# A two-layer decoder trunk on one core: opening, raw chunks, keys' diagonal and the place of an inverse

## The chip, the cores and the metric

The kernel runs on one core of one Trainium2 chip. The time is device microseconds of one execution, lower is better. A core has a matrix engine (TensorE, PE in the profile, with its weight loads as PEld), VectorE (DVE), ScalarE (ACT), GpSimd (POOL) and SyncE (SP), which issues the transfers here. Each engine takes its own instructions in order; they wait for one another through semaphores.

## The reference, cut to what matters

256 tokens of width 2048 go through two layers. All data are float32.

```python
for layer in range(2):
    h = rmsnorm(x, gains[0])
    m = even_mixer(h) if layer == 0 else rwkv7_time_mix(h)
    x = x + rmsnorm(m, gains[1])
    x = x + rmsnorm(swiglu(rmsnorm(x, gains[2])), gains[3])

def even_mixer(h):
    q, k, v, u = split(h @ w_in)          # 4 x 1024 columns
    return concat(diff_attention(q, k, v), s5(u)) @ w_out

def rwkv7_time_mix(x):                    # 32 heads of 64
    r, k, v = (mixed(x, j) @ w for j, w in ...)
    decay = exp(-exp(-softplus(-(w0 + tanh(xw @ w1) @ w2)) - 0.5))
    a = sigmoid(a0 + (xa @ a1) @ a2)
    # state S per head, over the 256 steps:
    # S = S * decay + (S @ -kk) outer (kk * a) + v outer k;  y = S @ r
```

The kernel computes the last recurrence in chunks of 64 steps. Each chunk and head needs the inverse T of a triangular 64x64 matrix made from the keys.

## The kernel before

**Weights.** They lie in memory as 776 chunks of eight 128x128 blocks (512 KB) in the order of use. `chunk_load` (L362 to L368) loads a chunk into `wr`; ScalarE rounds it into `wh` (L367) and VectorE subtracts, `wl` = `wr` − `wh` (L368). Each block is then multiplied in three passes (high by high, high by low, low by high) on L305. Each of the three tiles has three buffers. Some small tiles in the second mixer are taken "raw": `wr` alone, as one fp32 multiplication, without L367 and L368.

**Order.** A scheduler orders the instructions by priorities, but in the strict parts TensorE keeps program order. Whatever an engine waits for in its queue holds up all behind it.

**First mixer** (`even`). x and the first weights are loaded in the order of the table LX. x times its gain is split into 16 pairs of tiles `Z`; the same tiles of x are squared on ScalarE (L534), added on GpSimd (L536), and eight small matmuls give the norm. Four tiles of u go through the first eight chunks (`k_outer`). Then come the tiles of the list SEQ: v, q with k, u 4, u 5, and so on, one tile being two chunks. Beside it run the setup of the S5 layer (a long chain of small operations on VectorE, then tables S on GpSimd, L1001 to L1031), its products (VectorE L1059, GpSimd L1062 and L1063), and attention, which needs q and k copied out by VectorE (L711).

**Second mixer.** `rwkv_keys` goes through 16 head pairs j. For each, `gates` (L1568 to L1582) makes the decays and gates with ScalarE, VectorE and GpSimd; `pair` multiplies the keys. GpSimd copies a part of E (shown as H) into a block diagonal `bd` (L1629), TensorE multiplies it with the rest, VectorE masks the result into `ak` (L1633), and it is stored (L1635). After every eight pairs, `inverse` reads the stored `ak` into X (tiles XI, L1651) and runs one chain of 60 dependent VectorE operations (L1661, L1662) between an opening product (L1655) and a closing one (L1666), then stores the two diagonal quarters of the inverses. `inverse2` loads them again into A and W (tiles XI, L1681 to L1683), multiplies them in two steps of small matmuls, and stores the off-diagonal quarter (L1702). In a chunk, T is read back (L1836) and first used in the matmul shown as gs,T.

The call `slot("XI", 2, ...)` gives tiles from a ring of two buffers: X and XT of `inverse`, A and W of `inverse2`, all with the same name. The calls stand in this order: inverse of the first half after pair 8, inverse2 of the first half after the last pair, the first values (`wv`, group 0), inverse of the second half. Then `rwkv_values` starts with 20 units of fill work (values of the other groups) and the chunks; inverse2 of the second half comes in its seventh chunk.

Of the kernel before, what the change touches and what calls it, by code (L numbers as in the profile page):

```python
# [18 lines left out]
P = 128  # L19
T = 256  # L20
DM = 2048
# [17 lines left out]
I1 = 16  # L39
# [7 lines left out]
LX = ((0, 2), (0, 0), (2, 2), (4, 4), (1, 0), (8, 4), (2, 0), (12, 4))  # L47
# [12 lines left out]
BE = "g"  # L60
# [152 lines left out]
class Prog:  # L213
    def __init__(self, ctx, tc, d, layouts, dbg=None, stop=99):
# [4 lines left out]
        self.ahead = {}  # L219
# [31 lines left out]
    def load_const(self, key, t):  # L251
        lay, width = self.lay[key]
        self.nc.sync.dma_start(t, self.d[key])
        return {n: t[:, o:o + w] for n, (o, w) in lay.items()}
# [91 lines left out]

    def gated(self, ins):
# [10 lines left out]
    def chunk_load(self, c, raw=False, hp=None, pool=False):  # L358
        nc = self.nc
        with self.tc.high_priority(offset=HP if hp is None else hp):  # L360
            r = self.wp.tile([P, CB * P], F32, tag="wr", name=f"wr{c}")
            nc.sync.dma_start(r, self.d["wst"][c])  # L362
# [4 lines left out]
            self.gated(nc.scalar.copy(h, r))  # L367
# [43 lines left out]
    def tile(self, w, m, zH, zL, ks=None):  # L411
# [4 lines left out]
        for a, k in enumerate(ks):  # L416
            self.lab(w + str(m // 4))
            self.mmb(ps, w, k, m, zH[k], zL[k], a == 0, a == len(ks) - 1)
# [399 lines left out]
    def even(self):  # L818
        nc, v, gp = self.nc, self.nc.vector, self.nc.gpsimd
        with self.phase("ev"):  # L820
# [10 lines left out]
            ce = self.load_const("ce", self.slot("ce", 1, shape=[P, self.lay["ce"][1]]))  # L831
            acc = Prog.Acc(self)
            for k in range(KD):
                self.split(zH[k], zL[k], x[k], self.gain(0, 0, k))
                acc.add(x[k], k == KD - 1)
            r2 = self.slot("r2", 1, shape=[P, 2])
            _, R, R8 = self.rms_bc(acc.cur, half=0.125, col=r2)
            u = self.arr("U", 1, 8)
            us = self.k_outer([("in", 24 + a) for a in range(4)], zH, zL)
# [5 lines left out]
            mH, mL = self.arr("A", 2, 8, F32R), self.arr("A", 2, 8, F32R)  # L845
            yH, yL = self.arr("Y", 2, 8, F32R), self.arr("Y", 2, 8, F32R)
            lam = self.attn_setup(ce)
# [27 lines left out]
            def main():  # L875
                qk = {}
                for w, h in SEQ:
                    if w == "u":
                        ps = yield from self.tile("in", 24 + h, zH, zL)
                        self.evac_scaled(u[h], ps, R)  # L880
                        st["u"] += 1
                    elif w == "q":
                        q, k = self.tmp("q"), self.tmp("q")
                        ps = yield from self.tile("in", h, zH, zL)
                        self.evac_scaled(q, ps, R8)
                        ps = yield from self.tile("in", 8 + h, zH, zL)
# [93 lines left out]
    def s5_tables(self, cf, qt):  # L980
# [11 lines left out]
        nc.sync.dma_start(flat[:, 1024:], self.d["s5bc"][qt])  # L992
# [375 lines left out]
    def rwkv_consts(self, co):  # L1368
# [15 lines left out]
        co["S"] = cf[:, o + 192:o + 704].rearrange("p (j i) -> p j i", i=P)  # L1384
        self.nc.gpsimd.memset(co["S"], 0.0)
# [9 lines left out]
    def rwkv_keys(self, co, po, xs, x, m):  # L1395
# [128 lines left out]
        for j in range(16):  # L1524
# [24 lines left out]
    def gates(self, co, hid, j, Rd, gw, E):  # L1549
# [18 lines left out]
        v.tensor_scalar(ld, ld, e, e, op0=ALU.mult, op1=ALU.add)  # L1568
        v.tensor_tensor_scan(ld, co["reset"], ld, 0.0, op0=ALU.mult, op1=ALU.add)
        nc.scalar.activation(Pv, ld, AF.Exp)  # L1570
        nc.scalar.activation(iv, ld, AF.Exp, scale=-1.0)
        gp.memset(E[:, :, 0, 0, 0:1], 1.0)
        nc.scalar.activation(E[:, :, 0, 0, 1:], ch(ld)[:, :, :C - 1], AF.Exp)
# [3 lines left out]
        v.tensor_scalar(ta, ta, -0.5, -0.5, op0=ALU.mult, op1=ALU.add)  # L1577
        v.tensor_tensor(E[:, :, 1, 0], ch(ta), ch(iv), op=ALU.mult)
# [13 lines left out]
    def pair(self, co, kk, j, E):  # L1592
# [136 lines left out]
    def rwkv_values(self, co, po, vv):  # L1729
# [31 lines left out]
        self.strict = STRICT  # L1761
        with self.mid():
# [8 lines left out]
        fill(FI)  # L1771
        for s in range(NG * NC_):
# [5 lines left out]
            i2 = self.inverse2(co, po, 1, co["iv"]) if s == S2 else None  # L1778
# [250 lines left out]
```

## Time and profile before

| | |
|---|---|
| median of three runs | 2608.89 us (2600.57 to 2609.81) |
| the profiled execution | 2606.43 us, its span 2604.6 us |
| mean granted TensorE clock | 0.975 |
| busy: TensorE, VectorE, ScalarE, GpSimd | 95%, 63%, 46%, 16% |
| TensorE busy, 1548 to 1577 us | 19.6 of 29 us |

Read first the share of each engine, then a table of stretches: where TensorE is not busy for the whole stretch lies the time that a change can win. A row of a timeline gives the start, the duration, engine, line, operation, the tile written and those read, and in brackets how long the engine stood idle before it and what ended that. A line of a group has the count, the busy time and the mean of one in nanoseconds.

### The profile page before, as it was taken

Reading aid. Unit: us, or ns where it says so; the run is one execution under the profiler, and the core shown is the slowest. Engines: PE = TensorE matmul, PEld = TensorE weight load, DVE = VectorE, ACT = ScalarE, POOL = GpSimd, SP = SyncE. Lnnn points to the kernel's source line nnn. Section 1 sums busy time; section 2 is a strip of 40 time slices with the busy share of each in tenths; the row PEclk is TensorE's granted clock in tenths of the full one; section 3 lists DMA queues with packets and bytes.
Section 4 is the critical chain, followed back from the end, with each engine's and each line's share of the span. In section 5 each row is a group of like instructions: output and inputs, shape, how many; then the busy total and the mean of one; then the engine's idle time right before and its main releaser. Section 6 shows DMA issues by size and latency. Waiting matters only on the chain. (4 is left out here: it accounts for less than half of the span.)

```text
span 2604.6 us, 37350 instructions
## 1 busy us (share of the span) xinstructions
PE 2476.1 (95%) x14155; PEld 2081.8 (80%) x14155; DVE 1632.4 (63%) x2369; ACT 1205.3 (46%) x1808; POOL 408.3 (16%) x664
## 2 busy tenths in 40 slices
PE   7898799999999999998899889999999999999998
PEld 7786688788888888887799778887788888888886
DVE  7888985555555554445569978777555555555444
ACT  5343264644444444444666543443554444444433
POOL 4776621000000000000215630111100000000000
PEclk9898899999999999999999989999999999999999
DMA  6333256655555556664468677765555555555564
GB/s 218 114 114 103 80 178 199 203 187 186 192 187 186 192 186 200 200 224 161 154 216 248 206 224 197 207 200 171 202 187 186 189 190 186 186 190 190 194 206 162
DMA packets 221892, 481.93 MB, mean 185 GB/s; under 512 B 78736, under 2 KB 110736, under 8 KB 219920
## 3 DMA queue, kind: packets, MB, share of 16 engines
q1 hardware_dynamic: 221712, 479.55, 57.5%
q8 instruction: 111, 1.82, 0.3%
q14 instruction: 69, 0.57, 0.1%
HBM read 451.69 MB, written 27.79 MB: 184 GB/s over the span
## 5 line engine op out<-in xcount | busy, mean ns | idle before, releaser
L368 DVE TENSOR_TENSOR wl<-wr,wh 128x1024 fp32r<-128x1024 f32 x760 | 939.8, 1238 | 790.9 <-ACT wh L367 787.6
L367 ACT CAST wh<-wr 128x1024 fp32r<-128x1024 f32 x768 | 806.3, 1051 | 1023.7 <-PE pb L305 729.3
L305 PE MATMUL pg<-wh,Z 128*128 128x512 f32 x1664 | 641.2, 397 | 2.8 <-DVE Z L450 2.4
L305 PE MATMUL pb<-wh,Z 128*128 128x512 f32 x1408 | 554.0, 394 | 4.1 <-DVE Z L450 4.1
L305 PEld LDWEIGHTS pg<-wh,Z 128*128 128x128 f32 x1664 | 313.8, 189 | 72.8 <-issue 3.4
L305 PE MATMUL pg<-wl,Z 128*128 128x512 f32 x832 | 324.9, 391 | 0.4 <-DVE wl L368 0.4
L305 PEld LDWEIGHTS pb<-wh,Z 128*128 128x128 f32 x1408 | 264.9, 188 | 62.4 <-DVE Z L450 5.0
L305 PE MATMUL pb<-wl,Z 128*128 128x512 f32 x704 | 273.7, 389 | 0.0
L305 PE MATMUL pg<-wh,PP 128*128 128x512 f32 x576 | 225.6, 393 | 0.0
L305 PE MATMUL pb<-wh,PP 128*128 128x512 f32 x576 | 225.4, 393 | 0.0
L305 PEld LDWEIGHTS pg<-wl,Z 128*128 128x128 f32 x832 | 157.1, 189 | 34.5 <-DVE wl L368 1.2
L305 PE MATMUL pg<-wh,MX 128*128 128x512 f32 x504 | 174.9, 410 | 2.6 <-DVE X L1816 1.9
L305 PE MATMUL pg<-MX,wh 128*128 128x256 f32 x896 | 168.5, 286 | 6.7 <-ACT wh L367 4.0
L305 PE MATMUL pg<-Z,wh 128*128 128x256 f32 x736 | 146.3, 301 | 15.1 <-ACT wh L367 11.9
L305 PEld LDWEIGHTS pb<-wl,Z 128*128 128x128 f32 x704 | 132.5, 188 | 29.6
L305 PEld LDWEIGHTS pg<-MX,wh 128*128 128x128 f32 x896 | 139.9, 192 | 8.4 <-ACT wh L367 4.7
L305 PEld LDWEIGHTS pg<-Z,wh 128*128 128x128 f32 x736 | 120.5, 204 | 27.1 <-issue 14.8
L305 PE MATMUL pg<-MX,wl 128*128 128x256 f32 x448 | 128.1, 288 | 5.0 <-DVE wl L368 4.9
L305 PEld LDWEIGHTS pb<-wh,PP 128*128 128x128 f32 x576 | 108.2, 188 | 23.4
L305 PEld LDWEIGHTS pg<-wh,PP 128*128 128x128 f32 x576 | 108.2, 188 | 23.4
L500 POOL TENSOR_TENSOR ts<-ts,mhalf 128x1 f32<-128x1 f32 x6 | 3.3, 553 | 759.0 <-DVE ts L499 759.0
L305 PEld LDWEIGHTS pg<-wh,MX 128*128 128x128 f32 x504 | 96.7, 192 | 24.6 <-DVE X L1816 2.8
(429 smaller groups left out, 3639.1 us busy)
## 6 DMA issues: line engine op xcount, KB each, us to landing
wr<-wst SPq DMA_DIRECT2D x776, 512.0 KB, 3.4
dr<-H SPq DMA_DIRECT2D x16, 512.0 KB, 4.2
CH<-dr SPq DMA_DIRECT2D x16, 512.0 KB, 5.2
dr<-X SPq DMA_DIRECT2D x6, 1024.0 KB, 4.8
X<-dr SPq DMA_DIRECT2D x6, 1024.0 KB, 5.6
dr<-ak SPq DMA_DIRECT2D x16, 256.0 KB, 4.1
ln<-lnb SPq DMA_DIRECT2D x8, 512.0 KB, 4.7
S<-s5bc SPq DMA_DIRECT2D x4, 512.0 KB, 6.7
```

Source lines behind the costliest of these rows:

```text
L305: self.pe(self.nc.tensor.matmul(out, lhsT, rhs, start=start, stop=stop))
L367: self.gated(nc.scalar.copy(h, r))
L368: self.gated((nc.gpsimd if pool else nc.vector).tensor_tensor(l, r, h.bitcast(F32), op=ALU.subtract))
L500: self.nc.gpsimd.tensor_tensor(r, ms, self.mhalf[:, 0:1], op=ALU.pow)
```

## The change

Four parts.

1. **Opening.** A memset and 54 bf16 matmuls on a zeroed tile stand before the first real matmul, TensorE is strict from there, the splits of x are issued four steps ahead of the chunks, and chunk 1 is loaded before more of x. The norm comes from x by rows (two more loads of 1 MB, two ScalarE squares with an accumulated sum) instead of 16 squares, 14 additions and eight small matmuls. The constants `ce` and the S5 weights are tied behind chunks 5, 6 and 7.
2. **Raw chunks.** The first eight k-steps of ten tiles (u 4 to 7, q 0 to 2, k 0 to 2) are multiplied as fp32 from `wr` and from eight copies of x times gain (ScalarE, L887 of the new kernel, tiles Y). Ten chunks lose their cast and their subtraction.
3. **Keys.** `bd` is copied by ScalarE. In `gates` a VectorE operation becomes a ScalarE identity and two become one: 32 fewer on VectorE, 16 more on ScalarE.
4. **Inverse.** `inverse2` of the first half moves from the end of the keys, ahead of the first values, into the start of `rwkv_values`, behind the inverse of the second half, in three steps with 10, 5 and 5 units of fill work between. The condition I1 goes.

```diff
-LX = ((0, 2), (0, 0), (2, 2), (4, 4), (1, 0), (8, 4), (2, 0), (12, 4))
+LX = ((0, 2), (0, 0), (2, 2), (1, 0), (4, 4), (2, 0), (8, 4), (12, 4))
+W0 = 54
+NRAW = 3
-BE = "g"
+BE = "a"
...
+            z = (raw[k], None) if k < len(raw) else (zH[k], zL[k])
+            self.mmb(ps, w, k, m, *z, a == 0, a == len(ks) - 1)
...
+            self.warm(W0, cold)
+            for t in range(2):
+                self.behind(nc.scalar.activation(rows[t], rows[t], AF.Square, accum_out=ss[:, t:t + 1]), 4 + t)
...
-                        ps = yield from self.tile("in", 24 + h, zH, zL)
+                        ps = yield from self.tile("in", 24 + h, zH, zL, raw=raw)
-                        ps = yield from self.tile("in", h, zH, zL)
+                        ps = yield from self.tile("in", h, zH, zL, raw=raw if h < NRAW else [])
...
-        v.tensor_scalar(ld, ld, e, e, op0=ALU.mult, op1=ALU.add)
+        nc.scalar.activation(ld, ld, AF.Identity, bias=1.0)
-        v.tensor_scalar(ta, ta, -0.5, -0.5, op0=ALU.mult, op1=ALU.add)
-        v.tensor_tensor(E[:, :, 1, 0], ch(ta), ch(iv), op=ALU.mult)
+        v.scalar_tensor_tensor(E[:, :, 1, 0], ch(ta), 1.0, ch(iv), op0=ALU.add, op1=ALU.mult)
...
-            if j == I1:
-                with self.mid():
-                    list(self.inverse2(co, po, 0, iv))
-        if I1 > 15:
-            with self.mid():
-                list(self.inverse2(co, po, 0, iv))
         for _ in self.values(vv, 0, Vs[:, 0]):
             pass
         with self.mid():
-            co["iv"] = self.inverse(co, po, 1)
+            co["iv"] = [iv, self.inverse(co, po, 1)]
...
+        i2 = self.inverse2(co, po, 0, co["iv"][0])
+        with self.mid():
+            next(i2)
+        fill(FI // 2)
+        with self.mid():
+            next(i2)
+        fill(FI // 4)
+        with self.mid():
+            list(i2)
+        fill(FI // 4)
         with self.mid():
             cur = self.chunk_in(co, 0, 0, V)
...
-        fill(FI)
```

Where instructions move, three places. First SyncE's queue at the inverses. Before, around the end of the first values (XI1428 and XI1429 are the first inverse's tiles, XI1538 and XI1539 are A and W of the first inverse2):

```order
L1665 DMA dr1202_11618<-XI1428_13653 64x32x32 x2
L362 DMA wr457_15063<-wst 128x1024
L1669 DMA dr1432_13728<-XI1429_13654 64x1024
L1681 DMA XI1538_14621<-dr1200_11616 32x16x32 x4
L362 DMA wr458_15081<-wst 128x1024
L1682 DMA XI1538_14621<-dr1432_13728 32x16x32
L1683 DMA XI1539_14622<-dr1202_11618 32x16x32
```

and, at the same place in the changed kernel, where XI1528 and XI1529 are the second inverse's tiles, and XI1539 and XI1540 now are A and W:

```order
L371 DMA wr462_15053<-wst 128x1024
L1702 DMA dr1191_11441<-XI1528_14575 64x32x32 x2
L1706 DMA dr1532_14650<-XI1529_14576 64x1024
L1718 DMA XI1539_14670<-dr1188_11438 32x16x32
L1719 DMA XI1539_14670<-dr1420_13540 32x16x32
L1720 DMA XI1540_14671<-dr1190_11440 32x16x32
```

The loads of A and W stood behind the first inverse's stores; they now stand behind the second inverse's.

Second, VectorE's queue there. Before, after the last `ak` (MU and MV belong to the first chunk, XI1544 to the second inverse):

```order
L1633 TENSOR_TENSOR ak1536_14611<-pa1537_14614,M1195_11605 128x512
L368 TENSOR_TENSOR wl458_15084<-wr458_15081,wh458_15083 128x1024
L1944 COPY fs1600_15337<-M1195_11605 128x8
L1854 TENSOR_TENSOR MU1559_15030<-pa1558_15025,M1195_11605 64x512
L1857 TENSOR_TENSOR MV1557_15018<-pa1558_15025,M1195_11605 64x4x64 x2
L1655 TENSOR_TENSOR XI1544_14919<-XI1544_14919,dl1547_14926 128x1024
```

and now (XI1528 is the second inverse's X):

```order
L1670 TENSOR_TENSOR ak1524_14417<-pa1525_14420,M1183_11426 128x512
L1764 COPY X1236_12129<-pg1527_14428 128x512
L379 TENSOR_TENSOR wl458_14861<-wr458_14858,wh458_14860 128x1024
L1990 COPY fs1588_15143<-M1183_11426 128x8
L379 TENSOR_TENSOR wl459_14917<-wr459_14914,wh459_14916 128x1024
L1692 TENSOR_TENSOR XI1528_14575<-XI1528_14575,dl1531_14582 128x1024
```

The second inverse stood behind the first chunk's MU and MV, with weight subtractions among its operations; it now stands ahead of them, with none between its operations.

Third, VectorE's queue in the first mixer. Before, at the first S5 products (s, L1059) and the copy of the first q (L711):

```order
L1059 TENSOR_TENSOR s2226_1061<-pg224_1055,S119_611 128x512
L733 SCALAR_TENSOR_TENSOR sm170_733<-sm169_731,sm161_713 128x2
L1059 TENSOR_TENSOR s2227_1062<-pg224_1055,S119_611 128x512
L1059 TENSOR_TENSOR s2228_1069<-pb225_1056,S119_611 128x512
L1059 TENSOR_TENSOR s2229_1070<-pb225_1056,S119_611 128x512
L733 SCALAR_TENSOR_TENSOR sm171_735<-sm170_733,sm161_713 128x2
L736 TENSOR_SCALAR sm172_737<-sm160_712 128x2
L711 TENSOR_TENSOR q185_908<-pg187_910,n31_211 128x256
```

and now, where the same products are L1101 and the copy is L723:

```order
L379 TENSOR_TENSOR wl19_1099<-wr19_1096,wh19_1098 128x1024
L1017 TENSOR_TENSOR k24_452<-sm105_618,sm99_607 128x32
L379 TENSOR_TENSOR wl21_1225<-wr21_1222,wh21_1224 128x1024
L723 TENSOR_TENSOR q173_929<-pg175_931,n23_449 128x256
L1037 TENSOR_SCALAR s177_968<-S176_966 128x256
L1171 TENSOR_REDUCE sm143_719<-t142_717 128x2
L733 TENSOR_SCALAR sm147_724<-sm143_719 128x2
L1101 TENSOR_TENSOR s2214_1062<-pg212_1056,S106_623 128x512
```

The copy of the first q has moved ahead of the first S5 products; the subtractions of chunks 18 and 20 are gone from there, and the end of the S5 setup (L1017) stands between those of 19 and 21.

More of the change, by code (lines that the diff above doesn't have):

```diff
@@ L218, in __init__ @@
         self.strict, self.xw = False, []
-        self.ahead = {}
+        self.ahead, self.chunks = {}, {}
         self.alias = {}
@@ L345, in after, with behind @@
                                reason="order")
+    def behind(self, ins, c):
+        for a in self.chunks[c]:
+            if a.ins.engine == ins.ins.engine:
+                self.after(ins.ins, a.ins)
     def gated(self, ins):
@@ L830, in even, with part @@
             zH, zL = self.arr("Z", 4, 16, F32R), self.arr("Z", 4, 16, F32R)
[L831 to L839 removed]
+            self.strict = STRICT
+            u = self.arr("U", 1, 8)
+            cold = u[7][:, :P].bitcast(BF16)
+            gp.memset(cold, 0.0)
+            self.warm(W0, cold)
+            r2, ss = self.slot("r2", 1, shape=[P, 2]), self.slot("ssx", 1, shape=[P, 2])
+            xr = [self.mslots() for _ in range(2)]
+            rows = self.halves(xr)
+            steps = self.k_steps([("in", 24 + a) for a in range(4)], zH, zL)
+            def part(k):
+                self.split(zH[k], zL[k], x[k], self.gain(0, 0, k))
+            for k in range(4):
+                part(k)
+            for k in range(KD):
+                us = next(steps)
+                if k + 4 < KD:
+                    part(k + 4)
+                if k in (6, 8):
+                    t = k // 2 - 3
+                    self.behind(nc.sync.dma_start(rows[t], self.d["cx"][:, t * DM:(t + 1) * DM]), 3 + t)
+                if k == 10:
+                    ce = self.load_const("ce", self.slot("ce", 1, shape=[P, self.lay["ce"][1]]), 5)
+            for t in range(2):
+                self.behind(nc.scalar.activation(rows[t], rows[t], AF.Square, accum_out=ss[:, t:t + 1]), 4 + t)
+            ms = self.tmp("ts", [P, 2])
+            v.tensor_scalar(ms, ss, 1.0 / DM, 1e-6, op0=ALU.mult, op1=ALU.add)
+            gp.tensor_tensor(r2, ms, self.mhalf, op=ALU.pow)
+            self.strict = False
+            pr = self.spread(r2)
+            R, R8 = self.tmp("n"), self.tmp("n")
+            nc.scalar.activation(R, pr, AF.Copy)
+            nc.scalar.activation(R8, pr, AF.Copy, scale=0.125)
             with self.tc.high_priority(offset=SET):
@@ L845, in even @@
             mH, mL = self.arr("A", 2, 8, F32R), self.arr("A", 2, 8, F32R)
+            lam = self.attn_setup(ce)
+            raw = self.arr("Y", 2, 8)
             yH, yL = self.arr("Y", 2, 8, F32R), self.arr("Y", 2, 8, F32R)
-            lam = self.attn_setup(ce)
+            for k in range(8):
+                nc.scalar.activation(raw[k], x[k], AF.Copy, scale=self.gain(0, 0, k))
             st = dict(u=4, qk=[], vn=0, att=0, pv=0, s5=0)
```

38 lines of the change are left out of this document (22 added, 16 removed).

## The prediction

> **What bounds the kernel now.** I read the page first, then the table of busy time by stretches of the span, then in the stretches that the change touches the waits and the timelines of TensorE (PE), VectorE (DVE) and the SyncE queue.
>
> ```profile
> PE 2476.1 (95%) x14155; PEld 2081.8 (80%) x14155; DVE 1632.4 (63%) x2369; ACT 1205.3 (46%) x1808; POOL 408.3 (16%) x664
> ```
>
> TensorE is busy for 95% of 2604.6 us. The profiled execution took 2606.43 us, 1.8 more than its span and 2.5 less than the median, 2608.89. I sum against 2606.43 and add nothing for the 2.5. The table by stretches (length, then busy time of PE, PEld, DVE, ACT, POOL; near the end the clock) shows where the missing 5% lies:
>
> ```profile
> 0.00:43.00 43.00, 29.46 (x202) 28.64 (x202) 32.96 (x84) 24.09 (x48) 12.46 (x23) 0.88 0.68 232
> ...
> 65.00:145.00 80.00, 67.28 (x502) 60.08 (x501) 70.16 (x161) 26.72 (x49) 60.57 (x126) 0.89 0.35 113
> 145.00:360.00 215.00, 184.11 (x1416) 150.22 (x1416) 186.87 (x384) 78.86 (x170) 130.75 (x199) 0.90 0.33 106
> ...
> 1400.00:1548.00 148.00, 134.21 (x1011) 124.12 (x1009) 136.51 (x266) 84.09 (x180) 78.39 (x93) 0.97 0.73 218
> 1548.00:1577.00 29.00, 19.62 (x320) 16.27 (x320) 12.47 (x29) 9.79 (x18) 2.20 (x5) 0.71 0.87 212
> ```
>
> The change touches only these. Idle PE is 13.5 us in the opening, 12.7 up to 145, 30.9 up to 360, 13.8 in the keys, 9.4 around the first inverse: this is all that any part can win, besides the clock. In the first mixer and the keys VectorE is nearly as full as TensorE.
>
> **Opening.** Rows of PE's timeline (start, duration):
>
> ```profile
> 9.07 1.65 PE L305 MATMUL pg<-Z,wh 128*128 128x256 f32 x6 [9.07 <-ACT wh L367]
> 16.46 1.65 PE L305 MATMUL pg<-Z,wh 128*128 128x256 f32 x6 [2.81 <-ACT wh L367]
> 20.20 1.01 PE L305 MATMUL pg<-Z,wl 128*128 128x256 f32 x3 [1.66 <-DVE wl L368]
> 26.91 0.28 PE L305 MATMUL pg<-Z,wl 128*128 128x256 f32 x1
> 27.27 0.28 PE L305 MATMUL pg<-Z,wl 128*128 128x256 f32 x1
> 27.74 0.95 PE L305 MATMUL pb<-inv,n 128*128 128x1 f32 x8
> 28.55 0.95 PE L305 MATMUL pg<-Z,wh 128*128 128x256 f32 x6
> ```
>
> A block of three matmuls takes 0.36 us (26.91 to 27.27), a chunk of eight 2.85. Six matmuls took 1.65 us after the wait of 2.81 and 0.95 us at 28.55, so the second chunk ran at half clock. The change warms PE before the first chunk, takes 16 squares from ScalarE, and drops the eight small matmuls for the norm (27.74 to 28.55, 0.8 us). With the second chunk ready by about 15 us, six more at 2.85 and some 5 us of it still at half clock, the tiles end near 38 instead of 43.03: −5. Everything in the first 43 us that waits for the first weights (9.07) stays. Without any clock gain it is −2.5, with all of it −7.5. The trace lets a gap of 2.81 us throttle the clock. [...]
>
> What the opening wins has to get past the S5 tables. GpSimd's chain of small products starts when VectorE has copied a cosine, runs without a break, and VectorE's S5 products wait for it, with the copy of q queued behind them:
>
> ```profile
> 54.33 0.35 POOL L1001 COPY S<-k 128x8 f32<-128x8 f32 x2 [0.31 <-DVE k L962]
> 85.43 1.29 DVE L1059 TENSOR_TENSOR s<-pb,S 128x512 f32<-128x512 f32 x2 [1.24 <-POOL M L1063]
> 86.88 0.41 DVE L711 TENSOR_TENSOR q<-pg,n 128x256 f32<-128x256 f32 x1
> 87.35 1.65 PE L305 MATMUL pa<-q,q 64*128 64x128 f32 x8 [6.28 <-DVE q L711]
> 123.59 1.65 PE L305 MATMUL pa<-q,q 64*128 64x128 f32 x8 [4.75 <-DVE q L711]
> ```
>
> In the new order the cosine copy stands behind the wl of chunk 17, which needs a buffer that PE frees late in the first values. The values start near 38, six chunks of 2.85 bring that to 55, the cast, the subtraction and ten small operations of 0.2 to 59: 4 to 6 later than 54.33 (I allow 1 either way), though PE is 5 earlier. So the wait of 6.28 at 87.35 grows, by about 2 (bounds 0 and +6).
>
> **Ten chunks in fp32.** The kernel already has this form elsewhere; the rows of it and of what is dropped:
>
> ```profile
> L305 PE MATMUL pg<-MX,wr 128*128 128x256 f32 x128 | 28.1, 380 | 1.2 <-POOL MX L1408 1.2
> L367 ACT CAST wh<-wr 128x1024 fp32r<-128x1024 f32 x768 | 806.3, 1051 | 1023.7 <-PE pb L305 729.3
> L368 DVE TENSOR_TENSOR wl<-wr,wh 128x1024 fp32r<-128x1024 f32 x760 | 939.8, 1238 | 790.9 <-ACT wh L367 787.6
> wr<-wst SPq DMA_DIRECT2D x776, 512.0 KB, 3.4
> ```
>
> Those are 64 blocks (two records each): 28.1/64 = 0.44 us against 0.36, so 80 blocks cost TensorE 80 × 0.08 = +6.4. VectorE loses 10 × 1.24 = 12.4 us, ScalarE 10.5 less eight copies of x. A raw buffer is freed by TensorE instead of VectorE, so the next-but-two load starts late: it has one split chunk and one raw chunk, 2.85 + 3.5 = 6.3 us, for landing (3.4, the last row), cast 1.05 and subtraction 1.24, together 5.7. That just holds; I book 0, with +6 as the bound (ten times 0.6).
>
> What VectorE's relief returns: six of the ten chunks lie before 123.59, 7.4 us, more than the 4.75 waited there. That wait goes (−4.75), two small ones of 0.67 and 0.90 too, and with them some of the clock (0.89 over 80 us, 8.8 us lost; I take 2.5 back). The first mixer up to 145: −5 + 2 + 6.4 − 4.75 − 1.6 − 2.5 = **−5**; bounds −13 and +7. From 145 to 360 nothing is removed; an earlier start moves all alike: 0 (±4).
>
> **Keys.** Rows of the timeline and of the sources:
>
> ```profile
> 1445.28 2.08 PE L305 MATMUL pa<-bd,H 128*128 128x128 f32 x8 [4.72 <-POOL bd L1629]
> L1629 POOL COPY bd<-H x32: 387/486/7919, 1371.2 to 1541.4; 64x256 f32<-64x256 f32 x32
> L1603 ACT COPY KR<-pg x16: 362/370/379, 1366.9 to 1521.9; 128x256 f32<-128x256 f32 x16
> L1568 DVE TENSOR_SCALAR m<-m x16: 232/280/849, 1358.8 to 1515.4; 128x256 f32<-128x256 f32 x16
> L1577 DVE TENSOR_SCALAR m<-m x16: 273/300/1837, 1361.4 to 1520.8; 128x256 f32<-128x256 f32 x16
> ```
>
> The diagonal copies go to ScalarE: 32 × 0.37 = 12 us, and 16 identities of some 0.4 us make 6; with 84 of 148 us busy it holds them. VectorE loses 16 × 0.28 + 16 × 0.30 = 9.3 of 136.5. The 4.72 us wait goes; of the rest (13.8 idle) I take 1.3: **−6**, bounds −13 (all idle) and +4 (copies behind the 1.05 us casts, one in four late by half a microsecond).
>
> **The first half's inverse moved behind the values.** This is the large term. Its two tiles A and W and the tiles X and XT of both inverses share two buffers. Before, A and W came between the two inverses; now the second inverse takes the buffers first. SyncE's queue, which runs in order, now holds the second inverse's stores ahead of the twelve loads of A and W, so TensorE's XI matmuls, held in program order after only 15 fill matmuls, wait for the whole second chain. Before, that chain ran on VectorE under fill work. Rows of the timelines of DVE, SP and PE, and how long the stores of ak took to land, and VectorE's busy time on these tiles from 1560 to 1635 (62 operations of the chain and its memset):
>
> ```profile
> 1537.61 2.03 DVE L1666 TENSOR_TENSOR XI<-XI,dl 64x1024 f32<-64x1024 f32 x1
> 1547.84 0.69 DVE L1633 TENSOR_TENSOR ak<-pa,M 128x512 f32<-128x512 f32 x1 [0.20 <-PE pa L305]
> 1566.51 1.23 DVE L1655 TENSOR_TENSOR XI<-XI,dl 128x1024 f32<-128x1024 f32 x1
> 1560.39 2.27 SPq L1651 DMA_DIRECT2D XI<-dr  x2
> DMA to landing us min/median/max: 2.0/4.1/7.6
> 1560.00:1635.00 75.00, 26.02 (x63) 0.94 0.74 196
> 1550.88 1.35 PE L305 MATMUL pb<-XI 32*32 32x32 f32 x122 [0.79 <-DMA XI<-dr]
> 1552.90 0.75 PE L305 MATMUL pb<-XI 32*32 32x32 f32 x38 [0.68 <-ACT XI L1691]
> 1558.32 0.25 PE L305 MATMUL pb<-XI 32*32 32x32 f32 x1 [4.03 <-issue]
> 1562.77 2.05 PE L305 MATMUL pa<-QB,CH 128*128 128x128 f32 x8 [2.48 <-DMA QB<-dr]
> 1576.99 1.14 PE L305 MATMUL pb<-gs,T 64*64 64x64 f32 x16
> ```
>
> Count from the last ak (1547.84), which the second inverse needs and which stands at the same place in both. To the first use of T (1576.99) it was 29.2 us. Now: ak 0.7; its store lands, 4.1; loads of X to the first operation, 1560.39 to 1566.51, 6.1; the chain 26.0; its last store, twelve loads and TensorE's main run, 1539.64 to 1550.88, 11.3; from there to T, 26.1 less the three waits of 0.68, 4.03 and 2.48, 18.9. Together 67.1: **+38**. The fill work between is the same 39 matmuls, so this is idle. Short end: a store landing in 2, loads usable in 4 and (my estimates both) 15 us behind the XI matmuls: 59, +30. Long end: 7.6 for the store, 13.3 and the full 26.1: 79.8, +50. VectorE is then free of the chain while the first values chunks run; the waits there are short: **−2** (0 to −4).
>
> Sum: 2606.4 − 5 − 6 + 38 − 2 = **2631**, 1% above the median.
>
> **Rivals.**
> - *VectorE is the bound of the first 360 us and of the keys.* It is busy 70.2 of 80, 186.9 of 215 and 136.5 of 148 us. If each microsecond taken from it there is one of time, and the saved waits also hold the clock up: −7.5 opening, −12.4 and as much again in clock and GpSimd's products, −13 keys, −2: −47, against a short stall of +30: **2590**, faster. It decides once the gains pass the stall. For it: the two waits for q behind VectorE's queue. Against: TensorE's idle time up to 145 is 12.7 us, with 6.4 added to it.
> - *A short stall and full gains at half that size*: −24 and +30, **2612**, no change. For it: queued stores often land in 2 us. Against: the chain's 26.0 alone nearly equals all that.
> - *Raw buffers free late*: ten split chunks each late by 0.6 to 1, as VectorE's queue holds wl behind S5 products; opening eaten by GpSimd's tables: +12 over the forecast, **2643**.
> - *The inverse does not wait* (loads served from other buffers): −13, **2593**. The order of the queue rules it out but for a misreading.
>
> **How the numbers follow.** Forecast 0.60, late buffers 0.12, no change 0.15, VectorE's bound 0.09, no wait 0.04. About 0.5% (13 us, so 2595.8 and 2621.9) can be told from no change. Of the forecast's case some 0.06 falls below 2621.9 (bounds of the stall and the gains together). Slower: 0.54 + 0.12 = 0.66; same: 0.06 + 0.15 = 0.21; faster: 0.09 + 0.04 = 0.13. The forecast's own range is 2616 to 2645; with no change and late buffers taken in, 2606 to 2648 leaves out about 0.2.
>
> **What would show it.** After the values' end PE stands idle for some 40 us in one piece, released by DMA XI<-dr or ACT, with VectorE running 62 XI operations without a wl among them. If that gap is under 25 us, the large term is wrong. PE's first S5 wait for q near 85 us still stands, the second near 120 is gone; raw matmuls start 0.22 us apart by record; no wait for bd stands in the keys, or it is put down to ACT. If the first 360 us come out more than 15 us shorter, VectorE was the bound and my step on the opening failed.

## The result and the profile after

The changed kernel takes 2629.86 us (median of four runs, 2628.50 to 2631.28), the kernel before 2607.3 (four runs, 2600.57 to 2609.81). The ratio is 1.0088 with a 95% interval of 1.0076 to 1.0100: slower by 0.9%, where 2631 was forecast. The profiled execution has a span of 2629.4 us against 2604.6, so 24.8 us are to be found.

Four marks divide both spans at places where the kernels do the same: the last matmul of `pg<-wh,A` that waited at the end of the first mixer ("mixer" below), the last `ak`, the first use of T, and the end.

| us | mixer | last ak | first T | span |
|---|---|---|---|---|
| before | 335.57 | 1547.84 | 1576.99 | 2604.6 |
| after | 336.28 | 1541.62 | 1604.13 | 2629.4 |
| after less before, up to here | +0.7 | −6.2 | +27.1 | +24.8 |
| the stretch alone | +0.7 | −6.9 | +33.4 | −2.3 |

First the page's line of busy times, after:

```profile
PE 2478.0 (94%) x14121; PEld 2077.1 (79%) x14121; DVE 1615.7 (61%) x2328; ACT 1214.1 (46%) x1842; POOL 358.0 (14%) x619
```

Each engine's sum is almost the same as before: TensorE 2478.0 against 2476.1. The loss is not more work but waiting. Where it lies, the table of stretches of after shows (length, busy time of PE, PEld, DVE, ACT, POOL, then the clock):

```profile
0.00:35.50 35.50, 31.48 (x241) 28.49 (x242) 21.53 (x57) 24.99 (x42) 1.40 (x10) 1.00 0.88 325
65.00:145.00 80.00, 65.34 (x401) 54.34 (x397) 64.92 (x151) 16.83 (x38) 54.12 (x131) 0.94 0.30 101
145.00:360.00 215.00, 182.42 (x1386) 147.83 (x1385) 183.59 (x382) 76.99 (x168) 128.55 (x198) 0.91 0.32 107
1400.00:1541.00 141.00, 130.91 (x1011) 122.01 (x1010) 131.47 (x244) 97.80 (x219) 57.59 (x69) 0.98 0.75 231
1541.00:1600.00 59.00, 17.05 (x312) 13.56 (x311) 31.26 (x73) 8.05 (x13) 3.61 (x6) 0.62 0.53 128
```

The last row is the large one: 17 of 59 us busy at clock 0.62. The keys (1400 to 1541) hold TensorE 93% busy instead of 91%. Between 65 and 145 VectorE has 5.2 us less to do than before, and TensorE, with 65 of 80, is no fuller for it. TensorE's timeline of after, at the places that the prediction named:

```profile
1.10 8.91 PE L315 MATMUL pa<-U 128*128 128x256 bf16 x54 [1.10 <-POOL U L846]
9.77 0.48 PE L308 MATMUL pg<-Z,wh 128*128 128x256 f32 x2
...
14.36 0.50 PE L308 MATMUL pg<-Z,wh 128*128 128x256 f32 x2 [1.62 <-ACT wh L377]
...
36.37 0.40 PE L308 MATMUL pg<-wh,Z 128*128 128x512 f32 x1
...
81.09 0.93 PE L308 MATMUL pa<-q,q 64*128 64x128 f32 x8 [4.44 <-DVE q L723]
81.95 2.86 PE L308 MATMUL pg<-Y,wr 128*128 128x256 f32 x6
...
123.13 1.23 PE L308 MATMUL pa<-q,q 64*128 64x128 f32 x6 [6.91 <-DVE q L723]
...
336.28 0.50 PE L308 MATMUL pg<-wh,A 128*128 128x512 f32 x1 [2.24 <-DVE q L723]
...
1582.60 0.28 PE L308 MATMUL pb<-XI 32*32 32x32 f32 x2 [36.29 <-DMA XI<-dr]
...
1587.80 1.88 PE L308 MATMUL pb<-XI 32*32 32x32 f32 x122 [1.28 <-DMA XI<-dr]
...
1604.13 1.11 PE L308 MATMUL pb<-gs,T 64*64 64x64 f32 x16 [1.53 <-DMA T<-dr]
```

The opening does what it should: behind the warm-up (1.10) the first matmuls at 9.77 and those behind a wait of 1.62 at 14.36 run at full clock (1.00 in the first row of the table), and the first tiles end at 36.37 where they ended at 43. But the second wait for q stands at 123.13 where it stood at 123.59, and is longer (6.91 against 4.75). By there the opening's gain is gone. At 1582.60 stands the gap the forecast was built on, 36.29 us in one piece, ended by a load of XI. The other engines' timelines of after give its working, VectorE's chain and SyncE's queue:

```profile
1541.62 0.69 DVE L1670 TENSOR_TENSOR ak<-pa,M 128x512 f32<-128x512 f32 x1
1551.05 1.23 DVE L1692 TENSOR_TENSOR XI<-XI,dl 128x1024 f32<-128x1024 f32 x1 [2.16 <-DMA XI<-dr]
1575.22 1.86 DVE L1703 TENSOR_TENSOR XI<-XI,dl 64x1024 f32<-64x1024 f32 x1
1594.93 1.23 DVE L379 TENSOR_TENSOR wl<-wr,wh 128x1024 fp32r<-128x1024 f32 x1 [17.84 <-ACT wh L377]
```

```profile
1546.26 2.06 SPq L1688 DMA_DIRECT2D XI<-dr  x2
1577.12 1.63 SPq L1706 DMA_DIRECT2D dr<-XI  x1
1580.10 0.34 SPq L1718 DMA_DIRECT2D XI<-dr  x1
```

The chain runs from 1551.05 to 1577.08 without anything else on VectorE, its store goes out at 1577.12, and only then, at 1580.10, the loads of A and W that TensorE waits for. SyncE's own waits there are 16.6 us for the chain, with the second inverse's first store at the head of its queue, and 1.3 us for a store to land, in front of the first load of A. Behind the chain VectorE itself idles 17.84 us, to 1594.93, until the next `wh` is cast: ScalarE stands 42.08 us, to 1589.71, for TensorE's XI matmuls and then 3.55 us more for TensorE's weight matmuls (pg) before that cast, so there is nothing to subtract.

### The profile page after: what moved, and what is told of

It is laid out like the page before. It is cut to its first block, busy times and chain, and to the rows that moved or that the text cites. A ratio compares the mean times of both kernels' runs of the same rounds, so it can differ in the third digit from the quotient of the medians.

```text
span 2629.4 us, 37168 instructions
## 1 busy us (share of the span) xinstructions
PE 2478.0 (94%) x14121; PEld 2077.1 (79%) x14121; DVE 1615.7 (61%) x2328; ACT 1214.1 (46%) x1842; POOL 358.0 (14%) x619
## 4 chain that ended last, share of the span: by engine, by line
PE 79%; DVE 10%; ACT 3%; POOL 3%; DMA 2%; issue 2%; SPq 0%; DVEq 0%; ACTq 0%; POOLq 0%
PE pg L308 44%; PE pb L308 32%; DVE wl L379 2%; PE pa L308 2%; DMA wr<-wst 1%; PE pa L711 1%; ACT wh L377 1%; DVE s L1101 1%; DVE XI L1698 1%; DVE M L1123 1%; DVE XI L1699 0%; DVE X L1123 0%; DVE s L1137 0%; ACT MX L1447 0%; DVE sm L1119 0%
## 5 line engine op out<-in xcount | busy, mean ns | idle before, releaser
L379 DVE TENSOR_TENSOR wl<-wr,wh 128x1024 fp32r<-128x1024 f32 x750 | 929.1, 1240 | 826.1 <-ACT wh L377 825.8
L377 ACT CAST wh<-wr 128x1024 fp32r<-128x1024 f32 x758 | 795.9, 1051 | 1015.6 <-PE pb L308 725.6
L308 PEld LDWEIGHTS pb<-wh,Z 128*128 128x128 f32 x1408 | 264.7, 188 | 62.5 <-DVE Z L462 5.0
L308 PEld LDWEIGHTS pg<-wl,Z 128*128 128x128 f32 x832 | 157.1, 189 | 34.5 <-DVE wl L379 1.2
L308 PE MATMUL pg<-Z,wh 128*128 128x256 f32 x576 | 113.3, 296 | 5.3 <-DVE s L1101 3.7
L308 PE MATMUL pg<-wl,PP 128*128 128x512 f32 x288 | 111.8, 388 | 0.0
L308 PE MATMUL pb<-wl,PP 128*128 128x512 f32 x288 | 111.7, 388 | 0.0
```

What stands on the lines that cost most here:

```text
L308: self.pe(self.nc.tensor.matmul(out, lhsT, rhs, start=start, stop=stop))
L377: ins.append(nc.scalar.copy(h, r))
L379: self.gated((nc.gpsimd if pool else nc.vector).tensor_tensor(l, r, h.bitcast(F32), op=ALU.subtract))
```

## The experiments

"Early loads" in the names below means that the loads of A and W stand again between the two inverses. All ratios are to the kernel before, each with its 95% interval. What every run gave at the four marks ("ak to T" is first T less last ak):

| kernel | mixer | last ak | first T | ak to T | span | ratio |
|---|---|---|---|---|---|---|
| before | 335.6 | 1547.8 | 1577.0 | 29.2 | 2604.6 | 1 |
| after | 336.3 | 1541.6 | 1604.1 | 62.5 | 2629.4 | 1.0088 |
| e1_inv_back | 337.0 | 1541.8 | 1576.3 | 34.5 | 2610.3 | 1.0001 |
| e2_inv_only | 338.0 | 1554.3 | 1618.0 | 63.8 | 2641.5 | 1.0120 |
| e3_inv_early_loads | 337.9 | 1545.8 | 1573.3 | 27.5 | 2601.7 | 0.9980 |
| e4_open_keys | 335.6 | 1542.0 | 1577.3 | 35.3 | 2604.4 | 0.9997 |
| e5_inv_back_late_second | 336.4 | 1546.0 | 1576.6 | 30.7 | 2603.1 | 0.9994 |
| e6_early_consts | 336.5 | 1547.5 | 1576.7 | 29.3 | 2607.8 | 0.9997 |
| e7_raw_only | 346.3 | 1563.6 | 1593.7 | 30.1 | 2628.2 | 1.0068 |
| e8_keys_only | 335.7 | 1543.4 | 1574.9 | 31.5 | 2604.1 | 0.9984 |
| e9_keys_early_loads | 339.4 | 1544.2 | 1571.6 | 27.4 | 2597.6 | 0.9963 |
| e10_open_only | 335.9 | 1551.7 | 1580.9 | 29.2 | 2610.1 | 1.0000 |
| e11_no_first_scan | 329.0 | 1536.3 | 1564.6 | 28.3 | 2592.2 | 0.9950 |
| e12_raw_late_copies | 341.2 | 1556.3 | 1583.5 | 27.2 | 2619.7 | 1.0053 |

A mark alone is good to about 2 us either way: before, e2, e8 and e9 have the same first mixer, and the mark is 335.6, 338.0, 335.7 and 339.4. What many rows share is firmer than any one.

**e1: after, with the first half's inverse2 put back.**

```diff
+        with self.mid():
+            list(self.inverse2(co, po, 0, iv))
         for _ in self.values(vv, 0, Vs[:, 0]):
...
-        i2 = self.inverse2(co, po, 0, co["iv"][0])
-        with self.mid():
-            next(i2)
-        fill(FI // 2)
...
+        fill(FI)
```

> The changed kernel with one part undone: inverse2 of the first half stands again at the end of the keys, ahead of the first values. Theory (shared ring of two buffers): the whole of the step at the inverses, -6 to +25.5 against before in the two traces, goes, so about 31 us less than the changed kernel, 2598, and the span from the last ak to the first use of T is near 29 us again. Rival (the step comes from the later matmuls having too little fill work, not from the ring): also back to 2598, which is why the next kernels are needed. Rival (the chain on VectorE costs as much wherever it stands): less than 10 us gained, 2620 or more.

2609.59 us, 1.0001 (0.9991 to 1.0011). The move is worth 1.0088 − 1.0001, some 23 us, but what is left is no gain: I had expected 2598. The keys' lead at ak, 6 us, is given back before T. TensorE's timeline and SyncE's queue of e1:

```profile
1562.48 0.77 PE L308 MATMUL pa<-QB,CH 128*128 128x128 f32 x2 [9.17 <-DMA QB<-dr]
...
1576.27 1.14 PE L308 MATMUL pb<-gs,T 64*64 64x64 f32 x16
```

```profile
1551.23 0.61 SPq L1884 DMA_DIRECT2D QB<-dr  x1
...
1553.39 5.17 SPq L1690 DMA_DIRECT2D XI<-dr  x2
1558.61 1.25 SPq L1885 DMA_DIRECT2D MV<-dr  x1
1559.90 0.62 SPq L1884 DMA_DIRECT2D QB<-dr  x1
```

The first load of QB went out at 1551.23, the second only at 1559.90. Between them stand a load of MV and, ahead of it, the second inverse's two loads of X: SyncE waited some 1.5 us before the first of these, 1.2 of it for TensorE's last XI matmuls, and the two then took 5.17 us to issue, against 2.27 before. Why the issue took so long is not traced. TensorE waits 9.17 us for QB, where before it waited 2.48.

**e2: before, with the move alone.**

```diff
-        if I1 > 15:
-            with self.mid():
-                list(self.inverse2(co, po, 0, iv))
         for _ in self.values(vv, 0, Vs[:, 0]):
...
+        i2 = self.inverse2(co, po, 0, co["iv"][0])
+        with self.mid():
+            next(i2)
+        fill(FI // 2)
...
-        fill(FI)
```

> The kernel before with this one part alone: inverse2 of the first half moved behind the inverse of the second. Theory: the path from the last ak to T grows from 29 to 62 us, so +33 on 2607, 2640, with one idle piece of TensorE of 36 to 41 us. Rival (the loss needs the freer queues of the other parts): under +20, below 2627.

2640.64, 1.0120 (1.0106 to 1.0134), as expected: the move alone costs 31 us. TensorE's timeline of e2 there:

```profile
1594.55 0.28 PE L305 MATMUL pb<-XI 32*32 32x32 f32 x2 [36.41 <-DMA XI<-dr]
...
1618.03 1.69 PE L305 MATMUL pb<-gs,T 64*64 64x64 f32 x16 [3.99 <-DMA T<-dr]
```

The same gap, 36.41 us, in a kernel with nothing else of the change.

**e3: after, with the loads of A and W early and the rest late.** The move stays (the matmul steps stand between the fills), only the loads come before the first values, ahead of the second inverse's tiles.

```diff
+        with self.mid():
+            co["iv"] = self.inverse2(co, po, 0, iv)
+            next(co["iv"])
         for _ in self.values(vv, 0, Vs[:, 0]):
             pass
-        with self.mid():
-            co["iv"] = [iv, self.inverse(co, po, 1)]
...
-        i2 = self.inverse2(co, po, 0, co["iv"][0])
-        with self.mid():
-            next(i2)
+        i2 = co["iv"]
...
             list(i2)
+            iv = self.inverse(co, po, 1)
```

> The changed kernel with A and W loaded ahead of the first values, their matmuls left where the change puts them (steps between the fill units), and the second inverse called after the last of these steps, so that the ring goes first half, A and W, second half again. Theory (ring): the long idle piece goes though the matmuls stay where the change has them; as the small waits between the steps are now filled, 0 to 6 us less than with the move undone, 2592 to 2598. Rival (too little fill work before the late matmuls, or the load queue after the values): an idle piece of over 20 us stays ahead of the XI matmuls, 2618 or more.

2603.51, 0.9980 (0.9972 to 0.9989): by the ratios 28 us ahead of after, 5 ahead of before. TensorE's timeline of e3:

```profile
1550.24 1.29 PE L308 MATMUL pb<-XI 32*32 32x32 f32 x128
...
1557.32 1.69 PE L308 MATMUL pb<-XI 32*32 32x32 f32 x128 [3.52 <-ACT XI L1729]
...
1573.29 1.94 PE L308 MATMUL pb<-gs,T 64*64 64x64 f32 x16 [5.25 <-DMA T<-dr]
```

The first XI matmuls wait for nothing, and the longest of the waits left is 5.25. So it was the place of the loads and the buffers, not the late place of the matmuls, that cost the time; the rival fell. Two things move together here, the loads of A and W and the second inverse behind them, so whether the ring of buffers alone or the order of SyncE's queue alone would have cost as much isn't separated. My figure was too low by some 6, of which 4.2 lie ahead of the last ak.

**e4: e1 without the raw chunks.**

```diff
-            raw = self.arr("Y", 2, 8)
-            for k in range(8):
-                nc.scalar.activation(raw[k], x[k], AF.Copy, scale=self.gain(0, 0, k))
...
-                        ps = yield from self.tile("in", 24 + h, zH, zL, raw=raw)
+                        ps = yield from self.tile("in", 24 + h, zH, zL)
```

> As the first of these kernels (move undone), and the ten raw chunks split again: what is left is the opening and the keys. Theory (the raw chunks cost TensorE 6 us and give back about as much in waits): within 3 us of the first, 2595 to 2601. Rival (VectorE is the bound of the first mixer, its relief of 12 us carries what the opening won): 6 to 12 us slower than the first, 2604 to 2610. Rival (their cost on TensorE comes on top and VectorE's relief gives nothing): 6 us faster, 2592.

2607.95, 0.9997 (0.9988 to 1.0006), against e1's 1.0001: beside the new opening the raw chunks neither give nor cost.

**e5: e1 with the second inverse called later,** behind the loads of the first chunk.

```diff
-        with self.mid():
-            co["iv"] = [iv, self.inverse(co, po, 1)]
...
             cur = self.chunk_in(co, 0, 0, V)
+            iv = self.inverse(co, po, 1)
```

> As e1 (move undone, the other three parts kept), and the second inverse is called behind the loads of the first chunk, so that its loads of X stand behind the first chunk's QB and MV in SyncE's queue, as in the kernel before; in e1 they had come ahead of them. Theory (the keys win 5 to 7 us up to the last ak and e1 gave them back because QB stood behind a load of X that waited for the ring): the wait of 9.2 us for QB shrinks to 2 to 4, about 5 to 6 us less than e1, 2603 against 2608 before. Rival (the keys' gain is lost in the transfers of the path itself, whatever the order of the queue): the same as e1, 2608 to 2610.

2607.21, 0.9994 (0.9985 to 1.0003). TensorE's timeline of e5:

```profile
1562.25 0.98 PE L308 MATMUL pa<-QB,CH 128*128 128x128 f32 x3 [4.27 <-DMA QB<-dr]
```

The wait shrinks from 9.17 to 4.27, but the matmul begins at 1562.25 against 1562.48: in this profile the last ak comes 4.2 us later than in e1 (1545.96 against 1541.80), and the XI matmuls behind it with it. From ak to T it takes 30.7 us against 34.5, so this path did get shorter, by 3.8. Over all the intervals overlap, so no gain is shown, and I had expected 5 to 6. That QB's load stood behind X's is shown by the queue; that this alone ate the keys' lead isn't.

**e6: e3 with the constants `ce` loaded earlier,** behind chunk 2 instead of 5.

```diff
-                if k == 10:
-                    ce = self.load_const("ce", self.slot("ce", 1, shape=[P, self.lay["ce"][1]]), 5)
+                if k == 4:
+                    ce = self.load_const("ce", self.slot("ce", 1, shape=[P, self.lay["ce"][1]]), 2)
```

> As e3, and the constants of the S5 setup are loaded behind chunk 2 instead of chunk 5. Theory (the chain of the S5 setup, tables and products paces the first mixer, and the opening's gain stands waiting for it): GpSimd's tables start near 50 instead of 58, and the mixer up to 360 us ends 4 to 6 us earlier, 2598 to 2600. Rival (VectorE's amount of work paces the mixer, not the start of the tables): within 1.5 us of e3, 2602 to 2605. Rival (the constants delay the weights of the opening): 2 us slower.

2607.78, 0.9997 (0.9988 to 1.0007). GpSimd's timeline of e6, the first copy of the S5 tables, and TensorE's at the second q:

```profile
49.99 0.35 POOL L1043 COPY S<-k 128x8 f32<-128x8 f32 x2
```

```profile
121.68 0.58 PE L308 MATMUL pa<-q,q 64*128 64x128 f32 x2 [5.53 <-DVE q L723]
```

The tables start 9.3 us earlier than in e3 (59.25), and the second q comes only 0.7 us earlier (122.39 in e3), with its wait still 5.53. VectorE's first S5 scan starts where it did, at 98.91 against 99.04. My theory, that the start of the tables sets the pace here, fell. The whole is some 4 us slower than e3, the way of the third case, but at the mixer's end e6 is not behind (336.5 against 337.9), so delayed weights in the opening don't explain it; the cause is open.

**e7: before, with the raw chunks alone.**

```diff
+NRAW = 3
...
+            z = (raw[k], None) if k < len(raw) else (zH[k], zL[k])
+            self.mmb(ps, w, k, m, *z, a == 0, a == len(ks) - 1)
...
+            for k in range(8):
+                nc.scalar.activation(raw[k], x[k], AF.Copy, scale=self.gain(0, 0, k))
```

> The kernel before with the ten raw chunks alone. Theory (their 6.4 us on TensorE fall into waits that the S5 chain sets): within 3 us of before, 2605 to 2611. Rival (VectorE's relief of 12 us carries): 5 us or more faster, below 2603. Rival (the raw price comes on top): 2613 to 2616.

2628.21, 1.0068 (1.0055 to 1.0082): 17.7 us slower, a plain miss. ScalarE's timeline of e7 in the opening:

```profile
10.47 0.89 ACT L852 ACTIVATE Y<-X,cg 128x256 f32<-128x256 f32 x2
13.48 1.69 ACT L852 ACTIVATE Y<-X,cg 128x256 f32<-128x256 f32 x4
...
17.28 1.03 ACT L368 CAST wh<-wr 128x1024 fp32r<-128x1024 f32 x1
```

The scheduler has put the copies, which nobody needs yet, ahead of the second chunk's cast, which came at 15.38 before. At the mixer's end e7 is 10.7 us late. e12 goes on from here.

**e8: before, with the keys' part alone.**

```diff
-BE = "g"
+BE = "a"
...
-        v.tensor_scalar(ld, ld, e, e, op0=ALU.mult, op1=ALU.add)
+        nc.scalar.activation(ld, ld, AF.Identity, bias=1.0)
...
-        v.tensor_scalar(ta, ta, -0.5, -0.5, op0=ALU.mult, op1=ALU.add)
-        v.tensor_tensor(E[:, :, 1, 0], ch(ta), ch(iv), op=ALU.mult)
+        v.scalar_tensor_tensor(E[:, :, 1, 0], ch(ta), 1.0, ch(iv), op0=ALU.add, op1=ALU.mult)
```

> The kernel before with the keys' part alone. Theory (5 us won up to the last ak, given back at the first chunk because the second inverse's loads move ahead of QB): within 2 us of before, 2606 to 2610. Rival (the keys' part is worth its 5 us by itself): 2602 to 2604.

2605.10, 0.9984 (0.9976 to 0.9993): 4.2 us gained, nearer to the rival's 5 than to my 2. The lead at ak is 4.4, of which 2.3 go before T to the same wait, 6.29 us in TensorE's timeline of e8:

```profile
1562.00 0.98 PE L305 MATMUL pa<-QB,CH 128*128 128x128 f32 x3 [6.29 <-DMA QB<-dr]
```

**e9: before, with the keys' part and the early loads of e3.** The diff is that of e8 and that of e3 together; opening and raw chunks stay out.

```diff
+BE = "a"
...
+        with self.mid():
+            co["iv"] = self.inverse2(co, po, 0, iv)
+            next(co["iv"])
         for _ in self.values(vv, 0, Vs[:, 0]):
...
             list(i2)
+            iv = self.inverse(co, po, 1)
```

> The kernel before with the keys' part and with A and W loaded ahead of the first values, their matmuls between the fill units and the second inverse called after them, as in e3; no new opening, no raw chunks. Theory (the keys are worth 4 us by e8, e3 puts the loads of the second inverse behind those of the first chunk and fills the waits between the steps): 5 to 9 us faster than before, 2600 to 2604, the fastest kernel so far. Rival (the opening and the raw chunks together carry part of e3's gain): as before or e8, 2605 to 2608.

2599.59, 0.9963 (0.9950 to 0.9976): 9.6 us faster than before and the best of the whole kernels. From ak to T it takes 27.4 us where before took 29.2 and e8 31.5, so the keys' lead is kept here.

**e10: before, with the new opening alone.**

```diff
+            self.warm(W0, cold)
...
+                self.behind(nc.scalar.activation(rows[t], rows[t], AF.Square, accum_out=ss[:, t:t + 1]), 4 + t)
```

> The kernel before with the new opening alone (the keys, the inverses and all weight chunks as before). Theory (the opening's 7 us are lost by the second wait for q, near 123 us): within 2 us of before. Rival (they are worth their 7 us): 2600 to 2603. Rival (the later S5 tables cost more than the opening wins): 2 to 5 us slower.

2610.0, 1.0000 (0.9989 to 1.0012). TensorE's timeline of e10 at the second q:

```profile
121.49 0.80 PE L308 MATMUL pa<-q,q 64*128 64x128 f32 x4 [4.63 <-DVE q L723]
```

Of 7 us won by 36 us, 2 are left at 121, and at the mixer's end (335.9 against 335.6) none.

**e11: e3 without the S5 scan of the first quarter.** Left out are its eight scans and what carries them over on VectorE; that quarter of the S5 output is therefore not computed.

```diff
-            if c:
+            if c and qt:
...
+            if qt:
-            v.tensor_tensor_scan(zc, rz.rearrange("p i j s -> p (i j s)"), zc, 0.0, op0=ALU.mult, op1=ALU.add)
+                v.tensor_tensor_scan(zc, rz.rearrange("p i j s -> p (i j s)"), zc, 0.0, op0=ALU.mult, op1=ALU.add)
```

> As e3, with the S5 scan of the first quarter left out (eight scans and their carries on VectorE, about 15 us; the output of that quarter is then not the reference's; the planner may order VectorE's queue anew). Theory (the opening's gain is lost because the second copy of q stands behind these operations in VectorE's queue): the wait near 123 us goes, TensorE passes that point 6 to 7 us earlier, and the whole takes 5 us or more less than e3. Rival (a later part of the S5 layer on VectorE and GpSimd sets the pace anyway): the wait near 123 goes, but the waits near 192 and later grow by as much, and the whole is within 2 us of e3.

2594.82, 0.9950 (0.9930 to 0.9969), some 8 us under e3. The rival fell: the first product of S5 that waits near 192 us in e3 comes 9.6 us earlier (183.13 against 192.74), with the same wait of 4.7. TensorE's timeline at the second q, e3 and then e11:

```profile
122.39 1.23 PE L308 MATMUL pa<-q,q 64*128 64x128 f32 x6 [6.16 <-DVE q L723]
```

```profile
116.62 0.93 PE L308 MATMUL pa<-q,q 64*128 64x128 f32 x8 [2.74 <-DVE q L723]
```

And the stretch from 100 to 123 us (PE, PEld, DVE and on), of before, of after and of e11:

```profile
100.00:123.00 23.00, 17.94 (x148) 16.74 (x146) 21.40 (x48) 8.17 (x15) 8.65 (x15) 0.97 0.46 154
```

```profile
100.00:123.00 23.00, 14.32 (x93) 12.14 (x91) 22.31 (x53) 4.75 (x12) 9.16 (x15) 0.93 0.25 92
```

```profile
100.00:123.00 23.00, 20.26 (x136) 17.09 (x136) 13.39 (x29) 7.13 (x21) 8.44 (x18) 1.00 0.34 124
```

In after VectorE is busy 22.31 of these 23 us, fuller than before though ten chunks in all lost their subtraction, and TensorE has 14.32 us of work left between its waits. With the scans gone VectorE falls to 13.39, TensorE rises to 20.26, and q comes 5.8 us earlier than in e3. VectorE's queue ahead of q sets the time here: the scans stand in it, and q's copy waits its turn. Its timeline shows from where to where, the first scan and the copy of the second q, before and then after:

```profile
105.63 1.46 DVE L1081 TENSOR_TENSOR_SCAN M<-rz,M 128x512 f32<-128x512 f32 x1 [1.18 <-POOL M L1063]
...
123.13 0.41 DVE L711 TENSOR_TENSOR q<-pg,n 128x256 f32<-128x256 f32 x1
```

```profile
98.14 3.06 DVE L1123 TENSOR_TENSOR_SCAN M<-rz,M 128x512 f32<-128x512 f32 x1 [2.64 <-POOL M L1105]
...
122.66 0.41 DVE L723 TENSOR_TENSOR q<-pg,n 128x256 f32<-128x256 f32 x1
```

Between these rows the timeline shows no wait. The scans start 7.5 us earlier in after, but seven of them stand ahead of this q, with three subtractions, where five stood before, with four. In the other kernels it is six without raw chunks behind the new opening (e4, e10), and seven or eight with raw chunks (e1, e3, e5; e6, e7, e12). As far as these counts show, the scheduler put scans where the subtractions had been. The kernel before without the scans was not run, so how much of e11's gain is the opening's, come through at last, stays open.

**e12: e7 with its copies late,** tied behind the eighth chunk's cast on ScalarE.

```diff
             for k in range(8):
-                nc.scalar.activation(raw[k], x[k], AF.Copy, scale=self.gain(0, 0, k))
+                i = nc.scalar.activation(raw[k], x[k], AF.Copy, scale=self.gain(0, 0, k))
+                self.after(i.ins, self.casts[7].ins)
```

> The kernel before with the ten raw chunks alone, as in the run that came out 17.7 us slower, but with the eight raw copies tied behind the eighth chunk's cast on ScalarE instead of ahead of the second's. Theory (the loss of the raw part alone came from its copies in ScalarE's queue in the opening, where the second chunk's cast waited for them, and from what that lateness does to the next 200 us): the second cast is back near 15 us, the first product of S5 near 192.5 is no later than 195 instead of 202.5, and the time is 2605 to 2614, within 5 us of before. Rival (the raw chunks' own price, 6.4 us of TensorE and raw buffers that come free late, makes it whatever the copies' place): the second cast is back near 15 us, but 202.5 is still above 198 and the time stays above 2618. If the mark near 192.5 is back and the time still above 2618, then the rest of the loss lies behind the first mixer and neither theory holds there.

2620.94, 1.0053 (1.0040 to 1.0067), 14 us slower than before; the intervals of e7 and e12 overlap a little, so I go by the marks. ScalarE's timeline of e12, and TensorE's at S5's product:

```profile
15.08 1.03 ACT L368 CAST wh<-wr 128x1024 fp32r<-128x1024 f32 x1
```

```profile
194.89 0.72 PE L306 MATMUL pg<-U,S 32*128 32x256 f32 x1 [5.00 <-DVE s L1066]
```

The cast is back (15.08), and so are nearly 8 of the 10 us at S5's product (202.52 in e7, 194.89 here, 192.54 before). At the mixer's end the profiles of e7 and e12 are 10.7 and 5.6 us behind before, at the last ak 15.8 and 8.4, at the end 23.6 and 15.1 (by the ratios the whole is 17.7 and 14). So it is the third case of the expectation: the copies' place explains half of the opening's loss, the raw chunks' own price (6.4 us of TensorE) about fits the rest up to the mixer's end, and 7 to 13 us of either lie behind it, in code that is the same as before's. What makes those stays open; that e4 and e1 do not differ says that they aren't a price of raw chunks as such.

## Why the prediction was right

The time and its main cause were right: the forecast's case came, for the reason given, and none of the rivals did. Point by point:

- **The moved inverse, +38: +33.4.** The gap, its releaser and its cover (15 of the 39 fill matmuls, then nothing) came as told; e2 shows that the move alone makes the gap, and e3 that it goes with the loads early and the matmuls left late. By steps, forecast and measured: ak 0.7 and 0.7; its store's landing, 4.1 and 3.9 (1542.33 to 1546.26); X's loads to the first operation, 6.1 and 4.8; the chain, 26.0 and 26.0; store and loads to TensorE's main run, 11.3 and 10.7 (1587.80); from there to T, 18.9 and 16.3. The chain's 26.0 is partly luck. I had taken its busy time of before, 26.02, as its length; alone on VectorE it was busy for 23.97 and took 26.03 from its first operation to its last end. The 2 us of gaps that I had left out are made up by three operations of 1.2 to 1.5 us in before, where after has one; their like take 0.2 to 0.4. The steps read from before, where more was being moved (DMA share 0.87 from 1548 to 1577, against 0.53 from 1541 to 1600 in after), were long by 0.2 to 2.6 each; that the traffic made them long was not shown.
- **Keys, −6: −6.9 from the mixer's end to the last ak.** The 4.72 us wait for `bd` is gone, in after and in e8. TensorE's idle time from 1400 to the end of the keys fell by 3.7 us (13.8 to 10.1), less than that wait, because its waits for `wl` grew from 4.0 to 6.7; its busy time fell by 3.3, at clock 0.98 instead of 0.97. So the size came, but only half of it by the waits I had counted. From the mixer's mark to ak, the nine kernels with this part take 1204.8 to 1211.0 us, the five without 1212.3 to 1217.3; means 1207.2 and 1215.4, so −8 over all. What I had not seen is that much of it is given back when the inverse stays where it was: 5.3 of 6 us in e1, 2.3 of 4.4 in e8.
- **After T, −2: −2.3.** In the span behind T, after and e2 (the two with the move) are the shortest of the fourteen, 1025.3 and 1023.5 us. The way fits, but e9 without the move has 1026.0 and before 1027.6, so a gain of 2 us is no more than the marks' own spread, and it is not shown.
- **Opening and raw chunks, −5: +0.7.** This is the step that failed, in its part "what VectorE's relief returns". The 4.75 us wait at 123.59 did not go but grew to 6.91. I had counted the subtractions that the raw chunks take from VectorE before 123 us as so much time for q. e6 ruled out the start of GpSimd's tables as the reason; e11 shows that VectorE's queue is, with the S5 scans in it: it is fuller in the last 23 us before q than it was, and seven scans stand ahead of q instead of five. Where another part of the freed time went, the waits of after between 40 and 145 us show (total, times, longest):

```profile
ACT wh L377 <- DMA wr<-wst: 32.9, 8, 7.9
...
DVE wl L379 <- ACT wh L377: 11.4, 8, 5.5
...
PE pa L308 <- DVE q L723: 11.3, 2, 6.9
```

In before the second of these was 3.5 us:

```profile
DVE wl L368 <- ACT wh L367: 3.5, 4, 1.5
```

So VectorE, which has 7.0 us less work between 40 and 145, waits 7.9 us more in front of subtractions whose weights arrive late. The +2 at the first q failed too: that wait shrank from 6.28 to 4.44. The opening's own estimate (tiles near 38) was short by 1.6: the clock stayed whole (1.00 over the first 35.5 us), where I had taken some 5 us at half clock. The clock that I took back did come as well, 0.94 instead of 0.89 between 65 and 145, and went into the same wait.

The two misses are of opposite sign, −5 that did not come and +38 that was 5 too big, so the sum is nearer to the measurement (1 us) than its terms deserve. On the rivals: "VectorE is the bound" is half true in the first mixer (e11), but the time that the edits freed on VectorE went to scans ahead of q and to waits for weights. "A short stall" was nearer with its stall than I was, 62.5 us against its 59 and my 67; it fell with its gains, of which it needed 24 us and got about 8.5. "Raw buffers free late" shows in ScalarE's 32.9 us, and through VectorE it may be part of the longer wait for q; but TensorE itself waits for no weight there, and the +12 did not come.

## What to carry to other kernels

When two users share a ring of buffers, moving one user's call moves it in the ring too: look at whose release its loads now wait for, and keep the loads early when only the computing has to be late (e3: 28 us). An in-order queue in which a load waits for a buffer, or is slow to issue, holds all loads behind it, so time won ahead of it can be lost there (e1: the two loads of X took 5.17 us to issue, the second load of QB went out at 1559.90 behind them, and TensorE waited 9.17 us for QB). Time taken from a busy engine came to nothing here unless it was taken between the engine's last wait and the result that others wait for (e11: the second q 5.8 us earlier than in e3), and the scheduler may fill what was freed with other work; ask which operations stand in that stretch after the change, not how full the engine is over 80 us.

## What the runs showed of the hardware

The clock did not follow the length of the last wait. In before, a wait of 2.81 us was followed by six matmuls at half rate (1.65 us, granted clock 0.50 from 16.4 to 19 us), and one of 2.48 us by eight at half rate (2.05 us at 1562.77, clock 0.50 from 1562.7 to 1564.8, against 1.05 for the same eight in after at 1596.59); in e11 a wait of 2.74 us was followed by full rate (0.93 us for eight at 116.62). In after, the first eight matmuls behind a wait of 4.44 us ran at full rate (0.93 us at 81.09, clock 1.00 from 81.0 to 81.9), where eight of the same form behind a wait of 4.75 took 1.65 us in before (123.59), and only the six raw ones behind them were slow (2.86 us at 81.95, clock 0.53 from 81.9 to 84.8, against 1.56 for six such matmuls in e12):

```profile
83.01 1.56 PE L306 MATMUL pg<-Y,wr 128*128 128x256 f32 x6 [2.37 <-DVE q L714]
```

So the 2.81 us ahead of the second chunk, which the prediction read as enough to throttle the clock, do not decide it by their length; what does is not shown.

The parts' prices do not add. Alone, opening, raw chunks, keys and move read 0, +17.7, −4.2 and +31 us, which is 45 together; the change has 23. Most of the surplus is the raw chunks' 17.7, which they cost beside the old opening and not beside the new one (e4 against e1).
